# A conditioned scale and shift (FiLM) on one core: slabs stored whole, projections loaded in halves

## The chip, the cores and the metric

The kernel runs on one core of a Trainium2 chip. Its time is the device time of one execution in microseconds (us). It is given as the median of several runs.

## What is computed

```python
batch, seq, dim = 32, 512, 256          # cond_dim = 64, all float32
gamma = conditioning @ gamma_proj       # [32, 64] @ [64, 256]
beta = conditioning @ beta_proj
out = x * (1 + gamma[:, None, :]) + beta[:, None, :]   # x: [32, 512, 256]
```

Each batch has one row of gamma and one of beta, 256 numbers each, and all 512 positions of the batch are scaled and shifted by them. x and the output are 16.78 MB each; the other inputs are 8 KB and twice 64 KB.

## The kernel before

**Tiling.** x is cut into four slabs of eight batches (`SLABS`, L29). A slab is a tile xs of 128 partitions with 32 rows of 256 numbers each (L56): partition p holds 32 neighbouring positions, which lie in memory as one run of 32 KB, and 16 partitions share a batch. All four slabs have their own buffer, so no load waits for a buffer to come free.

**Loads.** SP issues the loads of x (L60). Slab 0 comes in four DMAs of 8 rows (8 KB runs, `LOADS`, L38), the others in one each (32 KB runs). ACT issues the small inputs first: conditioning (L49), gamma_proj and beta_proj into the two halves of one tile gbproj of 64 partitions (L51 and L52).

**Gamma and beta.** An identity matrix, each column repeated 16 times (`rident`, L65 to L71), is multiplied with the conditioning on TensorE (L73), which spreads the transposed conditioning over the partitions of all slabs; DVE copies it to SBUF (L75). For each slab one matrix multiplication with gbproj (L80) gives gamma and beta for its 128 partitions in PSUM; it needs both projections. ACT writes a copy to SBUF, with 1 added to gamma (L83 and L86).

**The main loop** (L93 to L112) takes each slab in two groups of 16 rows. DVE does 11 rows of a group in two passes, (gamma + 1) * x (L101) and + beta (L104), and reads gamma and beta from PSUM; POOL does the other 5 with L103 and L105 and reads them from SBUF. All of it is in place, in xs. After a group ACT issues stores (L111) by the table `STORES` (L39): slabs 0 and 3 go out in two halves of 16 rows, one after each group (16 KB runs), slabs 1 and 2 whole, after their second group (32 KB runs).

**What sets the order.** Each engine works through its instructions in the order in which the program's build puts them. On POOL both multiplications of a slab stand ahead of its two additions; on the others the order is that of the code. SP and ACT have a DMA queue each, q1 and q10 in the profile, and both queues feed the same 16 DMA engines. The completion of DMAs is counted by eight semaphores, which the build hands out in turn, for both queues together. A DMA that takes a semaphore again waits until the DMA that had it before has landed: in this program SP issues slab 2 only after the first quarter of slab 0 has landed, and slab 3 only after beta_proj has.

Of the kernel before, what the change touches and what calls it, by code (L numbers as in the profile page):

```python
# [2 lines left out]

# [5 lines left out]


@with_exitstack
def kernel(
    ctx: ExitStack,
    tc: tile.TileContext,
    x: bass.AP,
    conditioning: bass.AP,
    gamma_proj: bass.AP,
    beta_proj: bass.AP,
    out: bass.AP,  # L20
):
    nc = tc.nc
    f32 = mybir.dt.float32
    ALU = mybir.AluOpType

    batch, seq, dim = x.shape
    cond_dim = conditioning.shape[1]
    P = 128
    SLABS = 4  # L29
    BS = batch // SLABS  # L30
    REP = P // BS
    ROWS = BS * seq // P
    assert SLABS * BS == batch and REP * BS == P and ROWS * REP == seq

    x_v = x.flatten_outer_dims().rearrange("(s p r) d -> s p r d", s=SLABS, p=P)
    o_v = out.flatten_outer_dims().rearrange("(s p r) d -> s p r d", s=SLABS, p=P)

    LOADS = {0: [8, 8, 8, 8]}  # L38
    STORES = {0: (16, 32), 1: (32,), 2: (32,), 3: (16, 32)}  # L39
    GROUP = 16  # L40
    ON_DVE = 11

    consts = ctx.enter_context(tc.tile_pool(name="consts", bufs=1))
    xpool = ctx.enter_context(tc.tile_pool(name="xpool", bufs=1))
    psum = ctx.enter_context(tc.tile_pool(name="psum", bufs=1, space=bass.MemoryType.PSUM))


    cond_s = consts.tile([batch, cond_dim], f32)
    nc.scalar.dma_start(out=cond_s, in_=conditioning)  # L49
    gbproj = consts.tile([cond_dim, 2 * dim], f32)  # L50
    nc.scalar.dma_start(out=gbproj[:, :dim], in_=gamma_proj)  # L51
    nc.scalar.dma_start(out=gbproj[:, dim:], in_=beta_proj)  # L52

    slabs = []
    for s in range(SLABS):
        xs = xpool.tile([P, ROWS, dim], f32, name=f"xs{s}")  # L56
        slabs.append(xs)
        r = 0
        for n in LOADS.get(s, [ROWS]):
            nc.sync.dma_start(out=xs[:, r : r + n, :], in_=x_v[s, :, r : r + n, :])  # L60
            r += n
        assert r == ROWS


    ident = consts.tile([batch, batch], f32)  # L65
    make_identity(nc, ident)
    rident = consts.tile([batch, batch * REP], f32)
    nc.vector.tensor_copy(  # L68
        out=rident.rearrange("p (b g) -> p b g", g=REP),
        in_=ident.to_broadcast([batch, batch, REP]),  # L70
    )  # L71
    cond_T_p = psum.tile([cond_dim, batch * REP], f32)
    nc.tensor.matmul(cond_T_p, lhsT=cond_s, rhs=rident, start=True, stop=True)  # L73
    cond_T = consts.tile([cond_dim, batch * REP], f32)
    nc.vector.tensor_copy(out=cond_T, in_=cond_T_p)  # L75

    gb_p, gb_s = [], []
    for s in range(SLABS):
        p_t = psum.tile([P, 2 * dim], f32, name=f"gb_p{s}")
        nc.tensor.matmul(p_t, lhsT=cond_T[:, s * P : (s + 1) * P], rhs=gbproj,  # L80
                         start=True, stop=True)
        s_t = consts.tile([P, 2 * dim], f32, name=f"gb_s{s}")
        nc.scalar.activation(out=s_t[:, :dim], in_=p_t[:, :dim],  # L83
                             func=mybir.ActivationFunctionType.Identity,
                             bias=1.0, scale=1.0)
        nc.scalar.copy(out=s_t[:, dim:], in_=p_t[:, dim:])  # L86
        gb_p.append(p_t)
        gb_s.append(s_t)

    def rows(t, n):  # L90
        return bass.AP(tensor=t.tensor, offset=t.offset, ap=[t.ap[0], [0, n], t.ap[1]])

    for s in range(SLABS):  # L93
        xs = slabs[s]
        g_p, b_p = gb_p[s][:, :dim], gb_p[s][:, dim:]
        g_s, b_s = gb_s[s][:, :dim], gb_s[s][:, dim:]
        for r0 in range(0, ROWS, GROUP):
            v = xs[:, r0 : r0 + ON_DVE, :]
            w = xs[:, r0 + ON_DVE : r0 + GROUP, :]
            nv, nw = ON_DVE, GROUP - ON_DVE  # L100
            nc.vector.scalar_tensor_tensor(out=v, in0=rows(g_p, nv), scalar=1.0, in1=v,  # L101
                                           op0=ALU.add, op1=ALU.mult)
            nc.gpsimd.tensor_tensor(out=w, in0=w, in1=rows(g_s, nw), op=ALU.mult)  # L103
            nc.vector.tensor_add(out=v, in0=v, in1=rows(b_p, nv))  # L104
            nc.gpsimd.tensor_tensor(out=w, in0=w, in1=rows(b_s, nw), op=ALU.add)  # L105
            done = r0 + GROUP
            if done in STORES[s]:
                e0 = 0
                for e1 in STORES[s]:
                    if r0 < e1 <= done or STORES[s] == (ROWS,):  # L110
                        nc.scalar.dma_start(out=o_v[s, :, e0:e1, :], in_=xs[:, e0:e1, :])  # L111
                    e0 = e1  # L112


# [1 line left out]
_INS = ['x', 'conditioning', 'gamma_proj', 'beta_proj']  # L116
_OUTS = [((32, 512, 256), 'float32')]


# [23 lines left out]
```

## Time and profile before

| what | us |
|---|---|
| median of 5 runs (lowest to highest) | 84.15 (83.88 to 84.71) |
| time of the profiled execution | 84.59 |
| span of the profiled execution, first to last instruction | 82.8 |
| busy: DVE / POOL / PE / ACT | 50.1 / 46.3 / 9.1 / 3.9 |
| one L101 or L104 on DVE (8 of each) | 3.09 |
| one L103 or L105 on POOL (8 of each) | 2.90 |
| first L101 starts / last L104 starts | 12.34 / 62.28 |
| landings of the slabs 1, 2, 3 | 23.3, 38.0, 52.9 |

The DMA engines moved 33.69 MB in 2080 packets, 407 GB/s over the span. A packet is one run of one partition here: 8, 16 or 32 KB for x and the output, 1 KB for a row of a projection, 4 bytes for a write to a semaphore, of which each of the 16 engines makes one for each DMA. The profile's first part gives each engine's busy time; its second cuts the span into 40 slices of 2.07 us and gives the busy share in tenths. The DMA queues are listed with packets, MB and the time that their packets took as a share of 16 engines. The chain of waits goes back from the last instruction of a compute engine to what released it, with start and duration in us. In the timeline, what ended an engine's idle time stands in brackets; several instructions of one line are merged, so a time there can be that of a whole group. The list of DMA issues ends with the us from issue to landing.

### The profile page before, as it was taken

How to read it: one execution, taken by the hardware profiler on the slowest of the kernel's cores; microseconds unless marked ns; L12 is line 12 of the kernel's file. 1: busy time of each engine (PE TensorE's matmuls, PEld its weight loads, DVE VectorE, ACT ScalarE, POOL GpSimd, SP SyncE). 2: the span in 40 equal slices, each digit the busy share in tenths (PEclk: the TensorE clock that was granted, in tenths of full speed). 3: DMA queues.
4: the chain of work that ended last, by engine and by line, in shares of the span. 5: the costliest groups of instructions: out<-in, count | busy, mean ns of one | idle time of the engine just before them, and what ended most of it. 6: DMA issues, size and time to landing. Idle time of an engine off the chain costs nothing.

```text
span 82.8 us, 155 instructions
## 1 busy us (share of the span) xinstructions
PE 9.1 (11%) x10; PEld 2.8 (3%) x10; DVE 50.1 (60%) x18; ACT 3.9 (5%) x9; POOL 46.3 (56%) x22
## 2 busy tenths in 40 slices
PE   0090399900000000000000000000000000000000
PEld 0010234100000000000000000000000000000000
DVE  2003009999999999985999993399999500000000
ACT  0600033330000000000000000000000000000000
POOL 2000019999999999905999990399999100000000
DMA  2899999989979999979999997998999799799990
GB/s 44 324 425 381 405 427 562 427 364 506 443 324 443 419 396 491 491 317 467 396 443 435 443 506 309 514 491 380 396 491 443 332 506 491 301 443 404 467 419 8
DMA packets 2080, 33.69 MB, mean 407 GB/s; under 512 B 288, under 2 KB 416, under 8 KB 416
## 3 DMA queue, kind: packets, MB, share of 16 engines
q1 hardware_dynamic: 1008, 16.78, 48.3%
q10 hardware_dynamic: 1072, 16.92, 47.7%
HBM read 16.92 MB, written 16.78 MB: 407 GB/s over the span
## 4 chain that ended last, share of the span: by engine, by line
DMA 62%; DVE 15%; ACTq 1%; issue 0%; DVEq 0%
DMA xs<-in_x_dram 52%; DMA gbproj<-in_beta_proj_dram 9%; DVE xs L104 7%; DVE xs L101 7%; ACTq L51 1%; ACTq L49 0%; DVEq L101 0%
## 5 line engine op out<-in xcount | busy, mean ns | idle before, releaser
L103 POOL TENSOR_TENSOR xs<-xs,gb_s 128x1280 f32<-128x1280 f32 x8 | 23.0, 2896 | 17.6 <-ACT gb_s L83 11.0
L101 DVE SCALAR_TENSOR_TENSOR xs<-gb_p,xs 128x2816 f32<-128x2816 f32 x8 | 24.7, 3086 | 9.2 <-ACT gb_s L86 5.5
L104 DVE TENSOR_TENSOR xs<-xs,gb_p 128x2816 f32<-128x2816 f32 x8 | 24.7, 3087 | 0.3
L105 POOL TENSOR_TENSOR xs<-xs,gb_s 128x1280 f32<-128x1280 f32 x8 | 23.0, 2896 | 0.0
L80 PE MATMUL gb_p<-gbproj,cond_T 64*128 64x512 f32 x8 | 7.2, 1073 | 3.4 <-DMA gbproj<-in_beta_proj_dram 3.4
L75 DVE COPY cond_T<-cond_T_p 64x512 f32<-64x512 f32 x1 | 0.7, 684 | 4.6 <-PE cond_T_p L73 4.6
L80 PEld LDWEIGHTS gb_p<-gbproj,cond_T 64*128 64x128 f32 x8 | 2.5, 326 | 8.2 <-issue 8.2
L73 PE MATMUL cond_T_p<-rident,cond_s 32*64 32x512 f32 x2 | 1.9, 1069 | 4.2 <-DMA cond_s<-in_conditioning_dram 4.2
L83 ACT ACTIVATE gb_s<-gb_p 128x256 f32<-128x256 f32 x4 | 1.5, 384 | 11.2 <-PE gb_p L80 11.2
L86 ACT COPY gb_s<-gb_p 128x256 f32<-128x256 f32 x4 | 1.5, 366 | 0.0
L83 ACT ACT_TABLE_LOAD x1 | 1.3, 1283 | 2.4 <-issue 2.4
L68 DVE COPY rident<-ident 32x512 f32<-32x512 f32 x1 | 0.4, 416 | 1.2 <-POOL ident masks.py:199 1.2
L73 PEld LDWEIGHTS cond_T_p<-rident,cond_s 32*64 32x64 f32 x2 | 0.3, 202 | 4.2 <-issue 4.2
masks.py:197 POOL MEMSET ident<- 32x32 f32 x1 | 0.1, 114 | 0.3 <-POOLq L127 0.3
masks.py:199 POOL TENSOR_SCALAR_AFFINE_SELECT ident<-ident 32x32 f32<-32x32 f32 x1 | 0.2, 203 | 0.1
L127 POOL MEMSET const-float32-0.0<- 128x1 f32 x1 | 0.1, 104 | 0.2 <-issue 0.2
L127 POOL MEMSET const-bfloat16-1.0<- 128x1 bf16 x1 | 0.1, 107 | 0.0
L127 POOL MEMSET const-uint8-127<- 128x1 uint8 x1 | 0.1, 107 | 0.0
L127 POOL MEMSET const-float32-1.0<- 128x1 f32 x1 | 0.1, 104 | 0.0
## 6 DMA issues: line engine op xcount, KB each, us to landing
xs<-in_x_dram SPq DMA_DIRECT2D x3, 4096.0 KB, 32.3
out_dram<-xs ACTq DMA_DIRECT2D x4, 2048.0 KB, 17.5
out_dram<-xs ACTq DMA_DIRECT2D x2, 4096.0 KB, 23.7
xs<-in_x_dram SPq DMA_DIRECT2D x4, 1024.0 KB, 8.7
gbproj<-in_gamma_proj_dram ACTq DMA_DIRECT2D x1, 64.0 KB, 6.7
gbproj<-in_beta_proj_dram ACTq DMA_DIRECT2D x1, 64.0 KB, 7.7
cond_s<-in_conditioning_dram ACTq DMA_DIRECT2D x1, 8.0 KB, 3.3
```

Of the source, the lines that this page charges most:

```text
L51: nc.scalar.dma_start(out=gbproj[:, :dim], in_=gamma_proj)
L68: nc.vector.tensor_copy(out=rident.rearrange("p (b g) -> p b g", g=REP), in_=ident.to_broadcast([batch, batch, REP]),)
L73: nc.tensor.matmul(cond_T_p, lhsT=cond_s, rhs=rident, start=True, stop=True)
L75: nc.vector.tensor_copy(out=cond_T, in_=cond_T_p)
L80: nc.tensor.matmul(p_t, lhsT=cond_T[:, s * P : (s + 1) * P], rhs=gbproj, start=True, stop=True)
L83: nc.scalar.activation(out=s_t[:, :dim], in_=p_t[:, :dim], func=mybir.ActivationFunctionType.Identity, bias=1.0, scale=1.0)
L86: nc.scalar.copy(out=s_t[:, dim:], in_=p_t[:, dim:])
L101: nc.vector.scalar_tensor_tensor(out=v, in0=rows(g_p, nv), scalar=1.0, in1=v, op0=ALU.add, op1=ALU.mult)
L103: nc.gpsimd.tensor_tensor(out=w, in0=w, in1=rows(g_s, nw), op=ALU.mult)
L104: nc.vector.tensor_add(out=v, in0=v, in1=rows(b_p, nv))
L105: nc.gpsimd.tensor_tensor(out=w, in0=w, in1=rows(b_s, nw), op=ALU.add)
L127: nc = _bacc.Bacc("TRN2", target_bir_lowering=False, num_devices=1)
```

## The change

Two tables of DMAs change. Slabs 0 and 3 are stored whole, each with one DMA after its second group, as slabs 1 and 2 were. Each projection is loaded with two DMAs of 32 rows in place of one of 64; ACT issues them in the order gamma, gamma, beta, beta. The loop over `STORES` is written in another way, but issues the same stores for a given table. The arithmetic stays as it is, with the same order on each engine.

```diff
-    STORES = {0: (16, 32), 1: (32,), 2: (32,), 3: (16, 32)}
+    STORES = {0: (32,), 1: (32,), 2: (32,), 3: (32,)}
...
-    nc.scalar.dma_start(out=gbproj[:, :dim], in_=gamma_proj)
-    nc.scalar.dma_start(out=gbproj[:, dim:], in_=beta_proj)
+    for half, proj in ((gbproj[:, :dim], gamma_proj), (gbproj[:, dim:], beta_proj)):
+        for c0 in range(0, cond_dim, 32):
+            nc.scalar.dma_start(out=half[c0 : c0 + 32, :], in_=proj[c0 : c0 + 32, :])
...
-            done = r0 + GROUP
-            if done in STORES[s]:
-                e0 = 0
-                for e1 in STORES[s]:
-                    if r0 < e1 <= done or STORES[s] == (ROWS,):
-                        nc.scalar.dma_start(out=o_v[s, :, e0:e1, :], in_=xs[:, e0:e1, :])
-                    e0 = e1
+
+            for e0, e1 in zip((0,) + STORES[s], STORES[s]):
+                if r0 < e1 <= r0 + GROUP:
+                    nc.scalar.dma_start(out=o_v[s, :, e0:e1, :], in_=xs[:, e0:e1, :])
```

Since the semaphores are handed out in turn, the two added DMAs move those of the later ones. In the changed program SP issues the last quarter of slab 0 after conditioning has landed, slab 1 after the first quarter of slab 0, slab 2 after the first half of gamma_proj and slab 3 after the first half of beta_proj. A line of the changed kernel has a number one higher than before from L52 to L104, so the matrix multiplication of L80 is L81 there.

More of the change, by code (lines that the diff above doesn't have):

```diff
@@ L105 @@
             nc.gpsimd.tensor_tensor(out=w, in0=w, in1=rows(b_s, nw), op=ALU.add)
-            done = r0 + GROUP
-            if done in STORES[s]:
-                e0 = 0
-                for e1 in STORES[s]:
-                    if r0 < e1 <= done or STORES[s] == (ROWS,):
-                        nc.scalar.dma_start(out=o_v[s, :, e0:e1, :], in_=xs[:, e0:e1, :])
-                    e0 = e1
+            for e0, e1 in zip((0,) + STORES[s], STORES[s]):
+                if r0 < e1 <= r0 + GROUP:
+                    nc.scalar.dma_start(out=o_v[s, :, e0:e1, :], in_=xs[:, e0:e1, :])
+        assert STORES[s][-1] == ROWS
 _INS = ['x', 'conditioning', 'gamma_proj', 'beta_proj']
```

## The prediction

> **What bounds the kernel now.** I read the page's first two parts, then the DMA traffic stretch by stretch, then the chain of waits and the issues, and last the timeline of DVE.
>
> ```profile
> span 82.8 us, 155 instructions
> ...
> PE 9.1 (11%) x10; PEld 2.8 (3%) x10; DVE 50.1 (60%) x18; ACT 3.9 (5%) x9; POOL 46.3 (56%) x22
> ...
> DMA  2899999989979999979999997998999799799990
> ...
> q1 hardware_dynamic: 1008, 16.78, 48.3%
> q10 hardware_dynamic: 1072, 16.92, 47.7%
> ```
>
> No engine is busy for more than 60% of the span, but the 16 DMA engines are full in nearly every slice; q1 (SP's, the loads of x) and q10 (ACT's: small inputs and stores) together fill 96%. So the kernel is bound by the DMA engines, and the question for any edit is whether it changes the DMA work or leaves the engines empty somewhere. The next answers are the DMA traffic in four stretches, packets, MB and share: 14 to 20 us (loads alone), 25 to 36 us (loads beside stores in 16 KB runs), 53 to 60 us (32 KB stores alone), 72 to 80 us (16 KB stores alone).
>
> ```profile
> q1 hardware_dynamic: 79, 2.59, 99.8%
> ...
> DMA packets 185, 4.60 MB, mean 419 GB/s; under 512 B 0, under 2 KB 0, under 8 KB 0
> ...
> q1 hardware_dynamic: 96, 3.15, 68.0%
> q10 hardware_dynamic: 89, 1.46, 30.9%
> ...
> q10 hardware_dynamic: 95, 3.11, 102.9%
> ...
> q10 hardware_dynamic: 226, 3.44, 100.4%
> ```
>
> A 32 KB load packet costs 0.998 x 6 x 16 / 79 = 1.21 us of one engine. A 16 KB store packet costs 1.004 x 8 x 16 / 210 = 0.61 (226 less 16 semaphore writes), a 32 KB store packet about twice that. The second stretch tells how two queues share: 96 packets of one to 89 of the other, so packet by packet, and the queue with the longer packets gets the bytes: 68% against 31%. Next the chain and the issues:
>
> ```profile
> 1.71 7.74 DMA gbproj<-in_beta_proj_dram
> ...
> 9.47 43.44 DMA xs<-in_x_dram
> ...
> 53.03 3.10 DVE xs L101
> ...
> gbproj<-in_gamma_proj_dram ACTq DMA_DIRECT2D x1, 64.0 KB, 6.7
> gbproj<-in_beta_proj_dram ACTq DMA_DIRECT2D x1, 64.0 KB, 7.7
> cond_s<-in_conditioning_dram ACTq DMA_DIRECT2D x1, 8.0 KB, 3.3
> ```
>
> The last slab lands at 52.9; its arithmetic and stores follow. The chain stops there, but the rings do not: the slices show DMA full up to 81 us. A chain that ends in DVE at 65.4 is not what the end waits for; a backlog of stores is. Last, the timeline of DVE and of store issues at the two places that move:
>
> ```profile
> 12.34 3.09 DVE L101 SCALAR_TENSOR_TENSOR xs<-gb_p,xs 128x2816 f32<-128x2816 f32 x1 [5.47 <-ACT gb_s L86]
> ...
> 20.76 45.03 ACTq L111 DMA_DIRECT2D out_dram<-xs  x6
> 21.59 3.09 DVE L104 TENSOR_TENSOR xs<-xs,gb_p 128x2816 f32<-128x2816 f32 x1
> ...
> 38.14 3.09 DVE L101 SCALAR_TENSOR_TENSOR xs<-gb_p,xs 128x2816 f32<-128x2816 f32 x1 [1.21 <-DMA xs<-in_x_dram]
> ...
> 53.03 3.09 DVE L101 SCALAR_TENSOR_TENSOR xs<-gb_p,xs 128x2816 f32<-128x2816 f32 x1 [2.57 <-DMA xs<-in_x_dram]
> ...
> 62.28 3.09 DVE L104 TENSOR_TENSOR xs<-xs,gb_p 128x2816 f32<-128x2816 f32 x1
> ```
>
> Slab 0 is done at 24.7, and its half stores are issued at 20.76 and 24.76; slab 3's at 61.68 and 65.46.
>
> **The change part by part.**
>
> *The same bytes in longer runs.* 512 packets of 16 KB become 256 of 32 KB. Per engine 32 x 0.612 = 19.6 us becomes 16 x 1.213 = 19.4: -0.2 at most, 0 at least, since records of neighbouring packets overlap by a few ns; I take -0.1. Four stores for six save two semaphore packets an engine, four projection loads for two add two, of 9 ns each: nothing.
>
> *The projections.* Per engine, gamma and beta are now 4 packets of 1 KB and a semaphore write each; after, 2 and a semaphore write, four times: 12 turns for 10. Beta lands 9.4 - 7.9 = 1.55 us after gamma, five turns of 0.31, the length of one 8 KB load packet served between two turns. Two more turns: the last piece lands 0.6 us later, at 10.0. Bounds: 0 if a semaphore write takes no turn; for the upper end the farthest row is the 3.8 us between the landings of cond_s (4.0) and gamma (7.9): two more DMAs at 3.8 give +7.7. I take 0.6, since the gamma-to-beta row is the same queue, place and size. ACT issues two more DMAs of 0.4 to 0.6 us; behind them only the table load (2.36, 1.28 us) waits, and ACT has nothing to do then until 11.66. What waits for the last piece is PE's first L80, and so DVE and POOL: they start at 12.9 instead of 12.3. It costs nothing, as it is a delay of arithmetic under full DMA engines.
>
> Here a rule speaks against the change. The Trainium skill, DMA: Bandwidth & Descriptors, Rules for kernel authors, advises against splitting a transfer into disjoint partition halves, as they serialise, and the same page puts the fixed cost of one DMA at about 2 us (measured for GpSimd's path). By that the landing would be 4 us later, an estimate from that page; by the row above 0.6. By either the sum stays as it is.
>
> *SP's queue.* In the built program, eight completion semaphores serve all DMAs in turn, so two more DMAs shift who waits for whom: slab 0's last quarter now waits for cond_s (4.0), slab 1 for the first quarter (5.7), slab 2 for gamma's first half (about 7), slab 3 for beta's first half (about 9). The rings work on slab 0 until 12.9 and on slab 1 until 22.9 (it lands at 2.7 + 20.6 = 23.3), so each is queued in time: 0. The rival below bounds it from above.
>
> *Slab 0's store.* Its first half went at 20.76 and no store packet shows before 24.1: 3.4 to 4.7 us, the loads already in front. After: the whole slab at 24.76 + 0.6 = 25.4, first packets at about 29.4. Until then loads alone run at the same rate, so cost 0. Slab 2 lands earlier: by 29.4 an engine has done (29.4 - 22.9) / 1.213 = 5.4 of its 8 packets, and the 1.2 us wait at 38.14 goes. What is late next is slab 3: from 29.4 on, 10.6 loads are left, and each now takes a turn beside a 32 KB store, 2.43 us, or 2.45 with the loss that the mixed stretch shows (419 against 431 GB/s, part of it). They end at 29.4 + 26.0 = 55.4. The same arithmetic for before (14.3 loads left at 25.0, at 1.85) gives 51.5 where the landing is 52.9, so I add 1.4: slab 3 lands at 56.8, 3.9 later.
>
> *Slab 3's store.* From landing to the last issue took 65.46 - 52.91 = 12.55 us. After: one store at 69.4, in the rings about 1.0 later (SP's first load, issued at 0.74, moves its first packets at 1.77): 70.4. Is there still a backlog? At 55.4 an engine has done 10.6 store packets; slabs 0 to 2 are 24, so 13.4 are left, 16.2 us, until 71.6. Slack 1.2 us, where before the second-last store had slack of 9. If it holds, the cost is 0; beyond it each us is a us.
>
> *Sum:* -0.1 + 0 + 0 + 0 = -0.1 against the profiled execution: 84.59 (its span of 82.8 and 1.8 around it) becomes 84.5. That execution is 0.44 above the median of the runs, 84.15, so the forecast for the median is 84.05, rounded to **84.1 us**.
>
> **The rivals.**
> *Slower: the store queue runs dry before slab 3.* Place: after slab 2's last packet. For it: the slack fell from 9 to 1.2. Against: each packet of this stage is counted. No row shows 32 KB loads beside 32 KB stores; if the loads got 45% instead of half, each would take 2.70 us, end at 29.4 + 28.6 = 58.0, land at 59.4, and the store be in the rings at 73.0. Stores done by 58.0: (28.6 - 12.9) / 1.213 = 13.0; the other 11 last until 71.4. 1.6 us idle: 85.7. It decides from a landing of 58.0 on, and is over 1% from 58.9.
>
> *Faster: the mixed phase loses less.* In 25 to 36 us the engines moved 419 GB/s, against 431 to 434 alone: 11 x (1 - 419/432) = 0.35 us. The mixed phase now starts 4 us later and has fewer packets; without that loss and with the full -0.2: 83.6. Against: the phase is as long as before, 26 us.
>
> *The projections are far later.* If the upper end of +7.7 held, DVE starts at 20.0 and works 49.4 us (16 x 3.09): slab 3's store at 69.5, in the rings 70.5. Loads then run alone to 36, so the backlog still lasts to 71.4: 84.1 again. It decides only beyond +8.6, where each us costs one.
>
> **How the numbers follow.** About 1% (0.84 us) is what a measurement of this kernel can tell from no change, its five runs reaching from 83.88 to 84.71. Forecast 0.70 (0.66 within 1%, 0.02 on each side from the spread), its own range 83.7 to 84.6. Store queue dry 0.15: 0.11 slower, 0.04 too little to tell. Less loss 0.10: half beyond 1%. Late projections 0.05: 0.01 slower, the rest the same. Faster 0.07, within 1% 0.79, slower 0.14. The range takes in the less-loss case with the runs' spread, 83.5, and the dry queue to most of its price, 85.3.
>
> **What would show it.** Right: DMA full in every slice to 81 us; q10 with 816 packets (1072 less 256); first L81 of PE at about 10.2; the first store issued at 25.4; no DVE wait at slab 2; slab 3 landing at 56 to 57.5 and its store at 69 to 70; shares near 50:50 between 30 and 55. Wrong: a slice at 70 to 73 us with the DMA below 9, a store landing more than 11 us after the last issue's packets could start, or loads with clearly less than half. If DMA is full and the time still differs, the packet prices were wrong.

## The result and the profile after

The changed kernel takes 84.69 us (median of 54 runs, 84.42 to 87.24), the kernel before 84.49 us (median of 94 runs, 83.88 to 86.07; the five runs shown ahead of the prediction gave 84.15). The ratio is 1.0029, with a 95% interval from 1.0015 to 1.0044: 0.25 us slower, where -0.1 was forecast. The ratio leaves out the 9 and the 2 runs of a slower state, over 1.5% above the fastest of their kernel, and so differs a little from that of the medians. The time lies in the stated range, but the sign of the change is wrong. The lowest times tell more than the medians: 33 of the 94 runs of the kernel before are below 84.2, none of the 54 of the changed kernel is below 84.4.

The page of the changed kernel, first the busy share of the DMA engines in 40 slices, then ACT's queue:

```profile
span 82.9 us, 155 instructions
...
DMA  1899999979969979989979999997998999799890
...
q10 hardware_dynamic: 816, 16.92, 47.5%
```

The packets are as many as forecast (816), and the engines are as full as before. The chain of waits, start and duration in us:

```profile
2.11 6.87 DMA gbproj<-in_beta_proj_dram
...
8.99 48.88 DMA xs<-in_x_dram
...
57.99 3.10 DVE xs L102
```

The last slab lands at 57.87 instead of 52.91. The timeline at the places that moved, in brackets the idle time ahead of an instruction:

```profile
9.91 7.16 PE L81 MATMUL gb_p<-gbproj,cond_T 64*128 64x512 f32 x8 [3.73 <-DMA gbproj<-in_beta_proj_dram]
...
25.08 45.66 ACTq L110 DMA_DIRECT2D out_dram<-xs  x4
...
38.63 3.09 DVE L102 SCALAR_TENSOR_TENSOR xs<-gb_p,xs 128x2816 f32<-128x2816 f32 x1 [1.38 <-DMA xs<-in_x_dram]
...
57.99 3.09 DVE L102 SCALAR_TENSOR_TENSOR xs<-gb_p,xs 128x2816 f32<-128x2816 f32 x1 [7.03 <-DMA xs<-in_x_dram]
```

Slab 0's store goes at 25.08, the wait at slab 2 is still there (1.38 us), and DVE waits 7.03 us for slab 3. The DMA traffic of 36 to 53 us, packets, MB and share, shows both queues packet by packet with equal shares:

```profile
q1 hardware_dynamic: 128, 3.67, 50.0%
q10 hardware_dynamic: 128, 3.67, 50.0%
```

Where is the time? The stretch in which the first stores meet the loads differs. The DMA traffic of the kernel before from 23 to 27 us, where its first store packets are moved:

```profile
q1 hardware_dynamic: 35, 1.11, 65.9%
q10 hardware_dynamic: 28, 0.46, 26.7%
```

The same of the changed kernel from 27 to 31 us, where its first store packets are moved:

```profile
q1 hardware_dynamic: 32, 1.05, 76.4%
q10 hardware_dynamic: 16, 0.52, 30.3%
```

Before, 34 loads (one of the 35 packets is a semaphore write) took 0.659 x 64 engine-us: 1.24 each, near the undisturbed 1.21. After, 32 loads took 0.764 x 64: 1.53 each. That is 0.6 us lost on each of the 16 engines, in one place. I call what packets take beyond their undisturbed time, summed from 13 to 60 us and divided by 16 engines, the added packet time; it is worked out from the trace's packet records. It is 0.63 us in this profile and 0.25 in that of the kernel before. There only 0.06 of it falls in the 4 us from the first store packet on, and 0.17 later, most of it by 34 us.

### The profile page after: what moved, and what is told of

It is laid out like the page before. It is cut to its first block, busy times and chain, and to the rows that moved or that the text cites. A ratio compares the mean times of both kernels' runs of the same rounds, so it can differ in the third digit from the quotient of the medians.

```text
span 82.9 us, 155 instructions
## 1 busy us (share of the span) xinstructions
PE 9.1 (11%) x10; PEld 2.8 (3%) x10; DVE 50.1 (60%) x18; ACT 3.9 (5%) x9; POOL 46.3 (56%) x22
## 4 chain that ended last, share of the span: by engine, by line
DMA 67%; DVE 15%; ACTq 2%; issue 0%; DVEq 0%
DMA xs<-in_x_dram 59%; DMA gbproj<-in_beta_proj_dram 8%; DVE xs L105 7%; DVE xs L102 7%; ACTq L53 1%; ACTq L49 0%; DVEq L102 0%
## 5 line engine op out<-in xcount | busy, mean ns | idle before, releaser
L104 POOL TENSOR_TENSOR xs<-xs,gb_s 128x1280 f32<-128x1280 f32 x8 | 23.0, 2891 | 22.6 <-ACT gb_s L84 11.3
L81 PE MATMUL gb_p<-gbproj,cond_T 64*128 64x512 f32 x8 | 7.2, 1071 | 3.7 <-DMA gbproj<-in_beta_proj_dram 3.7
L81 PEld LDWEIGHTS gb_p<-gbproj,cond_T 64*128 64x128 f32 x8 | 2.5, 324 | 8.5 <-issue 8.5
```

## The experiments

Three theories stood at the start. "Turn": the loads stall when the rings turn from loads alone to loads and stores. "Dry": the one store of slab 3 comes when no other store is queued, so the kernel can't end earlier. "Projections": the added DMAs cost it. Each ratio below is to the kernel before on the same chip, with its 95% interval; each timed kernel has 12 runs. Several of these intervals only just leave out 1, so that the runs below 84.2, a third of those of the kernel before, are given as well.

**The parts one by one.** From the changed kernel, the stores put back:

```diff
-    STORES = {0: (32,), 1: (32,), 2: (32,), 3: (32,)}
+    STORES = {0: (16, 32), 1: (32,), 2: (32,), 3: (16, 32)}
```

> The projections in halves, all stores as before. Theory 'dry' (the whole store of slab 3 reaches the rings as the backlog ends, so the kernel cannot end earlier): same time as before, within 0.1 us. Theory 'turn' (the first whole store of slab 0 makes the loads stall longer when the rings turn to stores: 0.63 us an engine between 24 and 38 us against 0.21): same as before. Theory 'projections' (the two added DMAs and the shifted semaphores cost it): slower by 0.25 us, the whole difference.

Measured: 84.82 us, ratio 1.0042 (1.0009 to 1.0075). From the changed kernel, the projections put back (one DMA each), all slabs whole:

```diff
-    for half, proj in ((gbproj[:, :dim], gamma_proj), (gbproj[:, dim:], beta_proj)):
-        for c0 in range(0, cond_dim, 32):
-            nc.scalar.dma_start(out=half[c0 : c0 + 32, :], in_=proj[c0 : c0 + 32, :])
+    nc.scalar.dma_start(out=gbproj[:, :dim], in_=gamma_proj)
+    nc.scalar.dma_start(out=gbproj[:, dim:], in_=beta_proj)
```

> All slabs stored whole, projections as before. 'Dry' and 'turn': slower than before by 0.25 us. 'Projections': same as before within 0.1 us.

Measured: 84.82 us, ratio 1.0036 (1.0001 to 1.0070). As this one, with slab 3 in halves:

```diff
-    STORES = {0: (32,), 1: (32,), 2: (32,), 3: (32,)}
+    STORES = {0: (32,), 1: (32,), 2: (32,), 3: (16, 32)}
```

> Slab 0 whole, slab 3 in halves, projections as before. 'Dry': same as before or 0.1 us faster, since the first half of slab 3 is in the rings some 4 us before the backlog ends. 'Turn': slower by 0.3 us, with 0.6 us of added packet time an engine between 24 and 38 us. 'Projections': same.

Measured: 84.80 us, ratio 1.0046 (1.0011 to 1.0081). And with slab 0 in halves, slab 3 whole:

```diff
-    STORES = {0: (32,), 1: (32,), 2: (32,), 3: (32,)}
+    STORES = {0: (16, 32), 1: (32,), 2: (32,), 3: (32,)}
```

> Slab 0 in halves, slab 3 whole, projections as before. 'Dry': same as before: slab 3 lands at 53, its one store is issued at 65.5, and the backlog lasts to 71. 'Turn': same as before. A loss here would speak for something in the last store itself, such as its longer packets.

Measured: 84.69 us, ratio 0.9983 (0.9946 to 1.0021).

What follows: "dry" falls as the cause. Slab 3 whole costs nothing alone, and slab 0 whole costs all of it with slab 3 in halves.

The ratio of the projections in halves needs care, since much of it lies behind the last packet. At the end of the program SP waits for all semaphores, one or two at a time, in a fixed order. These are its semaphore instructions of the program's last line that end after 81.9 us, first of the kernel before, then with the projections in halves alone; two of them belong to the meeting of all engines that follows:

```profile
L138 SPq EVENT_SEMAPHORE  x3: 17/17/28, 82.0 to 82.8; - x3
L137 SPq EVENT_SEMAPHORE  x7: 17/28/41408, 40.7 to 83.1; - x7
```

In the kernel before, and in the changed kernel too, the last store's semaphore is in the last of these waits. With the projections in halves alone it is in an early one, and four more waits follow, at about 0.06 us each. From the last DMA packet to the end of the span pass 1.17 us in the kernel before, 1.16 in the changed kernel, but 1.47 here; it is 1.28 with all slabs whole and 1.24 with slab 0 or slab 3 alone whole. So 0.30 us (0.35%) of the 0.42% lies behind the last packet, and has nothing to do with the traffic; 0.07% (-0.26 to 0.40) is left. Of all slabs whole 0.23% is left (-0.12 to 0.57), of slab 0 whole 0.38% (0.03 to 0.73).

So "projections" falls as well, for all that these runs can tell. "Turn" as I had put it fits the times, but not the packets: with the projections in halves alone the packets lost 0.51 us an engine, where 0.2 was expected, and with 0.30 us taken off each of its runs still none is below 84.4. What this kernel and the one with slab 0 whole share is that the first store is issued later: at 21.44 and 24.69 us instead of 20.76. The DMA traffic where the first store packets are moved, first with the projections in halves alone, 24 to 28 us:

```profile
q1 hardware_dynamic: 32, 1.05, 71.6%
q10 hardware_dynamic: 22, 0.36, 21.0%
```

then with slab 0 whole alone, 27 to 31 us:

```profile
q1 hardware_dynamic: 32, 1.05, 77.8%
q10 hardware_dynamic: 16, 0.52, 30.3%
```

That is 1.43 and 1.56 us for a load packet. So the next theory was "time of the first store": what costs is the moment at which the first stores meet the loads.

**The moment moved alone.** One more operation on POOL in the kernel before, meant to delay the first store:

```diff
+    spare = consts.tile([P, dim], f32)
+    nc.gpsimd.tensor_tensor(out=spare, in0=gb_s[0][:, :dim], in1=gb_s[0][:, dim:], op=ALU.mult)
```

> The kernel before with one more multiplication on POOL (128x256, about 0.6 us) ahead of slab 0's additions, into a tile that nobody reads: the first store is issued at about 21.35 instead of 20.76, nothing else moves on the path. Theory 'turn by time' (what costs is at which moment the first stores meet the loads, and the projections in halves cost only because they delay that by 0.67 us): 0.3 us slower than before, with 0.4 to 0.5 us of added packet time an engine between 24 and 38 us. Rival 'projections' (the added DMAs cost by themselves): same as before, 0.2 us of added packet time.

The build put POOL's instructions in another order, with the first group's addition ahead of the second group's multiplication, and the first store was issued earlier, at 18.61. Measured: 84.46 us, ratio 0.9981 (0.9952 to 1.0010), the fastest run 84.34. So the expectation was not tested; an earlier store is no worse than before in the median, and has no runs below 84.2 either.

Both halves of slab 0 asked for after the second group:

```diff
-    STORES = {0: (16, 32), 1: (32,), 2: (32,), 3: (16, 32)}
+    STORES = {0: (32,), 1: (32,), 2: (32,), 3: (16, 32)}
...
+                    step = 16 if s == 0 else e1 - e0
+                    for f0 in range(e0, e1, step):
+                        nc.scalar.dma_start(out=o_v[s, :, f0:f0 + step, :],
+                                            in_=xs[:, f0:f0 + step, :])
```

> Slab 0 stored in two halves of 16 KB runs as before, but both issued after its second group, at 24.8. 'Turn by time': slower than before by 0.3 us, as with slab 0 whole, and 0.5 to 0.7 us of added packet time an engine. Rival 'run length' (the 32 KB packets of the first store make the stall): same as before, 0.2 us of added packet time.

ACT has nothing between the groups, so the build made the kernel before of it, with the first store at 20.78. Measured: 84.41 us, ratio 0.9981 (0.9948 to 1.0015). It is a repeat, and shows what 12 runs leave open: some 0.3%.

Then the first store was held back on ACT, by n small copies of a finished row ahead of it (in the kernel before):

```diff
+    spare = consts.tile([P, dim], f32)
...
+                        if s == 0 and e0 == 0:
+                            for _ in range(n):
+                                nc.scalar.copy(out=spare, in_=xs[:, 15, :])
                         nc.scalar.dma_start(out=o_v[s, :, e0:e1, :], in_=xs[:, e0:e1, :])
```

With two copies:

> The kernel before, with two small copies on ACT (128x256 of a finished row into a tile that nobody reads) ahead of the first store: it is issued at about 21.6 instead of 20.8. 'Time of the first store', in the form that the place inside a load packet of 1.21 us counts (stores first issued at 20.8 to 20.9 lost 0.05 to 0.2 us an engine, at 21.4 to 21.5 0.4 to 0.5): 0.3 to 0.5 us of added packet time, 0.2 to 0.3 us slower than before. 'Run length': 0.2 us of added packet time, same as before.

Measured: 84.51 us, ratio 1.0025 (1.0001 to 1.0049), none of the runs below 84.36. The profile shows 0.24 us of added packet time where 0.3 to 0.5 was expected, no more than that of the kernel before; it is of the fastest of the 12 runs. With three:

> As the run before this one with three copies: first store at about 22.0, one load packet (1.21 us) after 20.8. 'Time of the first store' by its place inside a packet: again at most 0.2 us of added packet time, and the time of the kernel before; by lateness alone: 0.4 us or more, slower by 0.3 us. 'Run length': same as before.

Measured: 84.70 us, ratio 1.0041 (1.0010 to 1.0071), none below 84.38. With one:

> The kernel before with one small copy on ACT ahead of the first store, issued at about 21.0 instead of 20.8; first stores at 21.3 (two copies) and at 22.05 (three) were 0.25 and 0.41% slower. 'Time of the first store' with a narrow good moment at 20.8 to 20.9: between before and two copies, +0.1%, with some runs still below 84.2. 'Any added work on ACT costs': as two copies, +0.25%, no run below 84.3.

Measured: 84.54 us, ratio 0.9993 (0.9956 to 1.0029), five of the 12 runs below 84.2. The timelines of ACT tell why, first with one copy:

```profile
20.64 0.41 ACT L114 COPY spare<-xs 128x256 f32<-128x256 f32 x1 [3.34 <-POOL xs L106]
20.73 4.24 ACTq L115 DMA_DIRECT2D out_dram<-xs  x2
```

then with two:

```profile
20.79 0.84 ACT L114 COPY spare<-xs 128x256 f32<-128x256 f32 x2 [3.34 <-POOL xs L106]
21.31 3.80 ACTq L115 DMA_DIRECT2D out_dram<-xs  x2
```

and with three:

```profile
21.09 1.28 ACT L114 COPY spare<-xs 128x256 f32<-128x256 f32 x3 [3.34 <-POOL xs L106]
22.05 3.36 ACTq L115 DMA_DIRECT2D out_dram<-xs  x2
```

ACT issues the DMA while its last copy still runs. With one copy nothing moved: the first store was issued at 20.73, and the time is that of the kernel before. So one copy costs nothing by itself, and the delay costs, as far as the intervals tell: 0.5 us of it 0.25%, 1.0 us of it 0.41%. That this price lies in the packets shows with three copies, not in the one profile with two. In the profiled run with three copies the projections landed late too, so that its first store, at 22.05, came 1.29 us after 20.76: one load packet. By "the place inside a packet" this should have brought the loss back to that of the kernel before; with 0.54 us of added packet time it didn't, so that form of the theory falls, as far as one profile shows it. The DMA traffic with three copies, 24 to 28 us:

```profile
q1 hardware_dynamic: 32, 1.05, 67.8%
q10 hardware_dynamic: 18, 0.29, 17.2%
```

A load packet takes 1.36 us. With one copy, 23 to 27 us, it takes 0.616 x 64 / 32 = 1.23:

```profile
q1 hardware_dynamic: 32, 1.05, 61.6%
q10 hardware_dynamic: 31, 0.51, 29.6%
```

**Run length against moment.** Slab 0's store held until the second group is done, by a zero made from that group and added to row 0, as two DMAs of 16 rows (step 16) or one of 32:

```diff
+                    if s == 0:
...
+                        nc.scalar.activation(out=zero, in_=xs[:, 26, 0:1], func=ident_f,
+                                             bias=0.0, scale=0.0)
+                        nc.scalar.activation(out=xs[:, 0, :], in_=xs[:, 0, :], func=ident_f,
+                                             bias=zero, scale=1.0)
+                    for f0 in range(e0, e1, step):
+                        nc.scalar.dma_start(out=o_v[s, :, f0:f0 + step, :],
+                                            in_=xs[:, f0:f0 + step, :])
```

> Slab 0 stored in two DMAs with 16 KB runs, but not before its second group is done: ACT makes a zero from a number of the second group and adds it to row 0, and rows 16 to 32 go first. First store at about 24.9, as in the kernel with slab 0 whole (24.7). 'Run length' (32 KB runs of the first store make the loads stall): same as before, at most 0.2 us of added packet time an engine between 24 and 38 us. 'Time of the first store': slower than before by 0.3 us, 0.5 to 0.7 us of added packet time, as with slab 0 whole.

Measured: first store at 24.97, 84.63 us, ratio 1.0023 (0.9997 to 1.0048), none of the runs below 84.38, 0.36 us of added packet time, most of it not at the first stores but from 32 to 34 us. Neither forecast is met.

> Slab 0 whole, as in the experiment with slab 0 alone, but the store held back by two small operations on ACT (a zero from the last group, added to row 0): issued at about 25.4 instead of 24.7. 'Run length': 0.65 us of added packet time an engine and the time of that experiment (0.3 us above before). 'Time of the first store' by its place inside a packet: 25.4 is 3.8 packets after 20.8, so less than 0.4 us of added packet time, and at most 0.1 us slower than before.

Measured: first store at 25.39, 84.77 us, ratio 1.0041 (1.0015 to 1.0068), none below 84.5, 0.46 us of added packet time; 0.07 us of its time lies in the waits at the end. By its place inside a packet it should have lost less than 0.4 us and been at most 0.1 us slower. Late stores with 16 KB packets lose the times below 84.2 too; whether 32 KB packets cost another 0.2% on top, these intervals leave open.

**More profiles of both kernels.**

> The kernel before once more, for its profile: its runs fall into two groups, near 84.1 and near 84.9. If the loss at the turn makes the groups, a profile with a time near 84.1 has at most 0.1 us of added packet time an engine between 24 and 38 us, one near 84.9 has 0.4 or more.

> As the run before this one: a second profile of the kernel before, to set its time against the added packet time between 24 and 38 us.

> The kernel before, for another profile. If the end is set by the one of the 16 DMA engines that lost most in the stretch where loads and stores run together, then the last store's 16 completions lie within 0.5 us of each other and begin at 80.8 in a run near 84.2, and end at 81.6 or later in a run above 84.6.

> The kernel before, for a fourth profile: the last store's 16 completions within 0.5 us from 80.8 on if the run is near 84.2, the latest at 81.6 or after if it is above 84.6.

> The changed kernel, for a second profile: time between 84.4 and 85.0; 0.5 to 0.7 us of added packet time an engine between 24 and 38 us as in its first profile; its fastest engine ends at 81.1 or later, where that of the kernel before ends at 80.8 to 81.0.

Measured, with the other profiled executions, in order of the first store (the end columns are those of the first and the last of the 16 DMA engines):

| kernel | first store at | added packet time | engines end | time, us |
|---|---|---|---|---|
| POOL order changed | 18.61 | 0.37 | 81.23 to 81.50 | 84.45 |
| one copy | 20.73 | 0.07 | 80.59 to 80.99 | 83.94 |
| before | 20.76 | 0.25 | 80.88 to 81.65 | 84.59 |
| before (late halves asked for) | 20.78 | 0.23 | 80.84 to 81.84 | 84.81 |
| before, fourth profile (b4) | 20.81 | 0.26 | 80.87 to 81.52 | 84.45 |
| slab 3 whole | 20.84 | 0.17 | 80.68 to 81.95 | 84.97 |
| before (b1) | 20.94 | 0.08 | 80.84 to 81.33 | 84.26 |
| before (b3) | 21.09 | 0.50 | 81.05 to 81.72 | 84.65 |
| two copies | 21.31 | 0.24 | 80.85 to 81.41 | 84.36 |
| projections in halves | 21.44 | 0.51 | 81.01 to 81.65 | 84.90 |
| before (b2) | 21.47 | 0.38 | 81.01 to 81.48 | 84.42 |
| three copies | 22.05 | 0.54 | 81.12 to 81.72 | 84.67 |
| slab 0 whole | 24.69 | 0.68 | 81.19 to 81.69 | 84.72 |
| all slabs whole | 24.91 | 0.68 | 81.25 to 81.73 | 84.79 |
| slab 0 late in halves | 24.97 | 0.36 | 81.18 to 81.63 | 84.58 |
| after | 25.09 | 0.63 | 81.12 to 81.75 | 84.68 |
| after (a2) | 25.11 | 0.55 | 81.19 to 81.93 | 84.88 |
| slab 0 whole, held | 25.39 | 0.46 | 81.03 to 81.85 | 84.87 |

The six with a first store from 20.73 to 20.94 lost 0.07 to 0.26 us an engine, mean 0.18; the five from 21.09 to 22.05 0.24 to 0.54, mean 0.43; the five with slab 0 whole 0.46 to 0.68, mean 0.60. Two profiles of the kernel before are in the middle group: its projections landed later there, with no edit. The time itself goes with the last engine's end: it is 2.93 to 2.97 us later in 13 of the 18 rows, and 3.02 to 3.25 in the five with more waits behind the last store. That end is the mean loss and the spread among the engines. The spread is 0.76 us on average in the six rows from 20.73 to 20.94 and 0.61 in the last six, which is how 0.4 us more of loss can go with 0.25 us of time. The expectation for b3 and b4 held in part: 81.72 goes with 84.65, but b4 began at 80.87 and spread to 81.52. That for b1 and b2 was wrong in its bounds: 0.38 us went with 84.42. That for a2 held.

What the table does not show is that the first store sets the time of a single execution. Among the six profiles of the kernel before (the repeat counted), 84.59 and 84.81 go with the earliest first stores, and 84.42 with the latest. The link is one between kernels: none of the 138 runs of the eight kernels with a later first store is below 84.2 (one would be without its longer waits at the end, 84.28 with all slabs whole). What makes a third of the runs of the kernel before so short stays open; none of its profiles is below 84.2.

## Why the prediction was wrong

- *What bounds the kernel* was right: in all of these kernels the DMA engines are full until the first of them ends, at 80.6 to 81.3 us.
- *The base.* 84.69 is 0.64 above the 84.05 of the sum. Of that, 0.34 is the base: the five runs ahead of the prediction had a median of 84.15, all 94 have 84.49. The rest is the sign of the change, and that the time lies in the range all the same is luck, as the range was made for other rivals.
- *The same bytes in longer runs*, -0.1: from the start of one packet to that of the next on the same engine a 16 KB store takes 0.607 us, one of 32 KB 1.210. So 32 x 0.607 = 19.42 became 16 x 1.210 = 19.36, -0.06.
- *The projections.* The landing 0.6 us later showed as 0.3 in this profile (first L81 at 9.91 for L80 at 9.59) and 0.7 in the one with the projections alone (10.26); the 15 profiles with one DMA for each projection reach from 9.44 to 10.29, so one pair of profiles says little. "It costs nothing, as it is a delay of arithmetic under full DMA engines" is not refuted by the 0.42% of the projections alone, of which 0.35% is the waits at the end; but the reason given doesn't hold, as a delay of the first store without split loads costs 0.25 to 0.41%. The skill's advice against disjoint partition halves, named in the prediction, agrees in its result, as the split gained nothing, though the few tenths of the landing are far from 4 us.
- *Slab 0's store* is the step of the sum that failed: "loads alone run at the same rate, so cost 0". The loads alone do, until the last ones ahead of the stores; the price is in the turn that follows, 0.63 us an engine in place of 0.25 in the two profiles. I had counted every packet at its undisturbed length and read the lower rate of the mixed stretch (419 against 431 GB/s) as a thing of the mix, the same for any start. It is a thing of the first ten us: from 38 us to the last load, still mixed, nothing is added in either kernel beyond 0.02 us. The rival of a mixed phase that loses less thus had the sign the wrong way round (and its 11 x (1 - 419/432) is 0.33, not 0.35). The last line of the prediction had named the case: DMA full and the time different, so the packet prices were wrong.
- *Slab 2 and slab 3.* "The 1.2 us wait at 38.14 goes" was wrong, it is 1.38, and slab 3 landed at 57.87, not 56.8, so its store went at 70.41, not 69.4. The sum had treated the 16 engines as one, but a slab lands with its last engine. On three engines the first store packet came 3.9 to 4.1 us after the issue, as reckoned, on the other 13 one load packet later, 5.2 to 5.5 us. So the three were behind with their loads: their semaphore writes for slab 2 came at 38.0 to 38.2 us and for slab 3 at 57.4 to 57.5, those of the 13 at 36.3 to 36.6 and 55.7 to 56.0. The shares of 50% and the one-for-one packets were right. The Trainium skill, DMA: Bandwidth & Descriptors, Queues, rings and completion order, has an engine drain a packet of typically 9 to 17 descriptors of one queue before it switches; 128 packets against 128, alternating in the records, say one run of 32 KB, and the measurement decides.
- *The rival of the dry queue* was nearly met: its limit was a landing at 58.0. The store of slab 3 found no other store queued. This is the answer of the changed kernel for that store:

```profile
DMA to landing us min/median/max: 11.7/11.7/11.7
```

Eight packets of 1.21 us and the 2 us around them are 11.7; before, the last store took 16.5, since it queued. The engines were empty for 0.02 us on average (0.07 in the second profile). So the slack of 1.2 us was used up and the price was still none, as the kernel with slab 0 alone whole shows: it has no dry queue and is as slow.

What stays open is why the turn is cheap at 20.7 to 20.9 and dear at most other moments. By these few profiles it is neither the run length alone nor the place inside a load packet.

## What to carry to other kernels

When the DMA engines are full from end to end, the time that is left is in the packets, not in the waits: compare the mean time of a packet, stretch by stretch, between two profiles before believing that a delayed transfer is free. A tuned kernel can owe some of its time to a moment that no line of the code names, here the issue of its first store, so an edit that only delays something well off the critical path can still move it. The spread of the runs is a result too: by the ratio the kernels differ by 0.25 us, by their fastest runs by 0.5. And an edit that adds DMAs can also reorder the waits at the end of the program: before a few tenths of a us are put down to the traffic, set the end of the last packet against the end of the span.

## What the hardware showed unexpectedly

Load packets of 32 KB took up to 1.97 us instead of 1.21 (2.17 in the second profile of the changed kernel) as the first store packets came, on most of the 16 engines at once, and nothing of the kind while loads ran alone (13 to 23 us: at most 0.02 us added in either kernel). In the changed kernel 0.53 of the 0.63 us lies in load packets that had started before the first store packet did. ACT issued a DMA behind a running copy without waiting for it: the copy of 0.4 us moved nothing, the second one 0.5 us. At the end of the program each wait of SP behind the last store took about 0.06 us, and their number, one to five in these kernels, followed from which semaphore the last store had.
